# Masked softmax on one core: other store sizes for the last six batches, and the last half store cut at partition 120

## The chip, the cores and the metric

The kernel runs on one core of a Trainium2 chip. The metric is device time in microseconds (us) of one execution, given as the median of seven runs. The profile is of one further execution; its "span" is the time from its first to its last instruction.

## The reference

The input is x of shape 16 x 8 x 256 x 256 (batch, heads, queries, keys) in 32-bit floats, and one length per batch. Along the key axis it is a softmax over the first `length` keys, and zero beyond:

```python
for b in range(batch):
    length = lengths[b]
    masked = x[b, :, :, :length].copy()
    masked = masked - np.max(masked, axis=-1, keepdims=True)
    exp_masked = np.exp(masked)
    result[b, :, :, :length] = exp_masked / np.sum(exp_masked, axis=-1, keepdims=True)
```

The lengths are drawn between 128 and 255. The output is the full 16 x 8 x 256 x 256 array, 33.55 MB, so every batch stores 2 MiB whatever its length.

## The kernel before

A batch has 2048 rows of 256 keys. They are laid on 128 partitions with 16 rows in each (`nt` = 16), so one partition holds 16 KiB of a batch, contiguous in the input and in the output. `half` is 8 of these rows. A tile `xt` has 12 slots of one batch each; batch b lies in slot b modulo 12, and all work is done in place.

Four queues and engines work side by side, and semaphores alone tie them together:

- SP issues the loads of batches 0 to 3 in full width (`load`, L96), then all stores. For each batch it waits on `s_out`, which counts finished half batches, and issues a store of rows 0 to 7 of every partition (8 KiB for each partition), then after a second wait two stores of four rows (4 KiB for each partition): `parts` (L47), the loop at L104 to L110. At the end it waits until the stores of batches 4 to 15, which share one semaphore, have all landed (L111; the profile puts this wait at L96).
- GpSimd (POOL) zeroes the columns from 160 on of the slots 4 to 11, then issues the loads of batches 4 to 15 (L136 to L141). Each load is only as wide as the batch's length, rounded up to one of a few widths (`pick`). For batches 12 to 15 it first waits until the stores of batches 0 to 3, whose slots they take, have landed, by the count `16 * len(parts)` (L140).
- The vector engine (DVE) builds a cap per batch (L167), takes the minimum of x and the cap so that masked keys become very negative (`clip`, L182), and later takes the reciprocal of the row sums (L207) and multiplies by it, half a batch at a time (L209). It takes the minimum of batch b + 1 before the multiplies of batch b. Each multiply raises `s_out` by one.
- The scalar engine (ACT) computes the exponential of one row in each partition at a time with the sum beside it (L225), and raises `s_exp` after each half.

A DMA of SP or of GpSimd is carried out by the core's 16 DMA engines, each of which takes its share of the partitions. Loads stand in one queue (q0 in the profile, those of GpSimd) and stores in another (q1, those of SP, which had the four first loads before them). Every DMA raises its semaphore by 16 in all.

The stores of a batch in the code before:

```python
parts = [slice(0, half), slice(half, half + half // 2), slice(half + half // 2, nt)]
```

Of the kernel before, what the change touches and what calls it, by code (L numbers as in the profile page):

```python
# [21 lines left out]
def kernel(  # L22
# [6 lines left out]
    nc = tc.nc  # L29
    P = nc.NUM_PARTITIONS  # L30

    batch, heads, seq_q, seq_k = x.shape
    rows = heads * seq_q
    assert rows % P == 0
    nt = rows // P
    half = nt // 2

    x_f = x.rearrange("b h q k -> b (h q) k").rearrange("b (p t) k -> b p t k", p=P)
    out_f = out.rearrange("b h q k -> b (h q) k").rearrange("b (p t) k -> b p t k", p=P)

    slots = min(12, batch)
# [2 lines left out]
    widths = list(range(160, 248, 8))  # L44
    low = widths[0]

    parts = [slice(0, half), slice(half, half + half // 2), slice(half + half // 2, nt)]  # L47
    mid = seq_k // 2

    pool = ctx.enter_context(tc.tile_pool(name="all", bufs=1))  # L50
# [1 line left out]
    xt = pool.tile([P, slots, nt, seq_k], F32, name="xt")  # L52
# [12 lines left out]
    inv_sum = pool.tile([P, batch, nt], F32, name="inv_sum")  # L65
    warm = pool.tile([P, 1], F32, name="warm")

    with tc.tile_critical(no_gpsimd_drain=True):  # L68
        sem = lambda n: ctx.enter_context(nc.semaphore(n))
        s_word = sem("s_word")  # L70
        s_word_p = sem("s_word_p")
        s_ones = sem("s_ones")
# [4 lines left out]
        early = batch - slots  # L77
        s_st = [sem(f"s_st{b}") for b in range(early)] + [sem("s_st")] * slots
# [5 lines left out]
        s_out = sem("s_out")  # L84

        def length(engine, b):

            return nc.values_load(  # L88
                (word_p if engine == POOL else word)[0:1, 2 * b : 2 * b + 1],
                engines=[engine],  # L90
                skip_runtime_bounds_check_because="compared with constants, never an address",
            )
# [9 lines left out]
        for b in range(1, ahead):  # L102
            load(nc.sync, b, seq_k)
        for b in range(batch):  # L104
            for k, s in enumerate(parts):
                if k < 2:
                    nc.sync.wait_ge(s_out, 2 * b + k + 1)
                nc.sync.dma_start(
                    out=out_f[b, :, s, :], in_=xt[:, b % slots, s, :]
                ).then_inc(s_st[b], 16)  # L110
        nc.sync.wait_ge(s_st[-1], 16 * len(parts) * slots)  # L111

        def pick(v, b, ws):

            if len(ws) == 1:
                load(nc.gpsimd, b, ws[0])
                return
            m = (len(ws) - 1) // 2  # L120
            with nc.gpsimd.If(v <= ws[m]):  # L121
                pick(v, b, ws[: m + 1])
            with nc.gpsimd.Else():  # L123
                pick(v, b, ws[m + 1 :])
# [11 lines left out]
        for n in range(ahead, batch):  # L136
            if n < slots:
                nc.gpsimd.wait_ge(s_fill, n - ahead + 1)
            else:
                nc.gpsimd.wait_ge(s_st[n - slots], 16 * len(parts))  # L140
            pick(length(POOL, n), n, widths + [seq_k])  # L141


# [56 lines left out]
        for b in range(batch):  # L200
# [3 lines left out]
            for h in range(2):  # L204
                s = slice(h * half, (h + 1) * half)
# [4 lines left out]
                    out=t[:, s, :],  # L210
# [8 lines left out]
        for first, last in ((0, slots), (slots, batch)):  # L219
            with nc.Fori(first, last, 1, engines=[ACT]) as i:  # L220
                nc.scalar.wait_ge(s_min, i + 1)
                slot = i - first
                for j in range(nt):
                    e = xt[:, bass.ds(slot, 1), j, :]
                    ins = nc.scalar.activation(  # L225
                        out=e,
                        in_=e,
# [3 lines left out]
                    if (j + 1) % half == 0:  # L231
                        ins.then_inc(s_exp, 1)


# [1 line left out]
_INS = ['x', 'lengths']  # L236
_OUTS = [((16, 8, 256, 256), 'float32')]
# [25 lines left out]
```

The softmax here doesn't subtract the row's maximum and nothing guards it: scores larger than these inputs give would overflow.

## Time and profile before

| What | Value |
|---|---|
| Median of 7 runs | 158.39 us (158.01 to 158.63) |
| The profiled execution's own time | 158.44 us |
| Its span | 156.1 us |
| Vector engine busy | 121.6 us (78% of the span) |
| Scalar engine busy | 105.2 us (67%) |
| GpSimd busy | 25.0 us (16%) |
| Bytes moved by DMA | 62.11 MB, 398 GB/s in the mean |
| HBM read and written | 28.51 MB and 33.55 MB |
| Stores issued by SP | 16 of 1024 KB and 32 of 512 KB |
| First and last issue of a store | 18.6 us and 137.4 us after the span's start |

The profile's page gives the busy time of each engine, then the span in 40 equal slices in which a digit is the busy share in tenths; the row called DMA is the mean share of the 16 DMA engines. The view of waits says who waited for whom. The view of windows cuts the span into chosen stretches and gives the busy time of each engine in each, and at the end of the row the DMA share and the rate. The trace also keeps a record of every single DMA packet (its start, length, bytes and queue, without the number of the DMA engine).

### The profile page before, as it was taken

The page shows a single profiled execution, that of the slowest core. Times are in us where ns is not written, and L with a number is a line of the kernel's source. Part 1 is how long each engine was busy: PE and PEld are TensorE (multiplying, and loading weights), DVE is VectorE, ACT ScalarE, POOL GpSimd, SP SyncE. Part 2 cuts the span into 40 slices and gives each one's busy share as a digit, 9 for nine tenths or more (in the row PEclk, how much of TensorE's full clock was granted, in tenths as well). Part 3 has the DMA queues.
Part 4 walks back from the last instruction along what each step waited for, and adds up shares of the span by engine and source line. Part 5 has one row for each costly group of instructions (what it writes and reads, how often), then busy time and mean ns, then how long its engine had stood idle before and what let it go on. Part 6 is the DMA issues. An engine that isn't in the chain of part 4 may idle for free.

```text
span 156.1 us, 1177 instructions
## 1 busy us (share of the span) xinstructions
PE 0.2 (0%) x1; PEld 0.1 (0%) x1; DVE 121.6 (78%) x99; ACT 105.2 (67%) x514; POOL 25.0 (16%) x27
## 2 busy tenths in 40 slices
PE   0000000000000000000000000000000000000000
PEld 0000000000000000000000000000000000000000
DVE  2566999999999999949995999997977999910000
ACT  3009999896979797948888497979592989300000
POOL 5995045652002002010000000000000000000000
DMA  4999999999999999999999999999999999999990
GB/s 126 424 441 424 437 357 393 410 435 426 382 402 405 411 426 405 418 408 415 409 412 416 405 415 404 412 419 406 418 441 414 422 423 421 421 426 425 429 396 34
DMA packets 11607, 62.11 MB, mean 398 GB/s; under 512 B 1058, under 2 KB 1154, under 8 KB 8786
## 3 DMA queue, kind: packets, MB, share of 16 engines
q1 hardware_dynamic: 7488, 41.95, 65.7%
q0 software_dynamic: 4112, 20.12, 32.0%
q14 instruction: 5, 0.04, 0.1%
q10 hardware_dynamic: 2, 0.00, 0.0%
HBM read 28.51 MB, written 33.55 MB: 397 GB/s over the span
## 4 chain that ended last, share of the span: by engine, by line
DVE 33%; DMA 29%; issue 12%; POOL 6%; another core or an unknown queue 4%; POOLq 1%; SPq 1%; DVEq 0%
DMA xt<-in_x_dram 29%; DVE xt L209 18%; DVE xt L182 12%; POOL xt L133 4%; POOL xt L96 2%; DVE inv_sum L207 1%; DVE cap L167 1%; POOLq L88 1%; SPq L96 1%; POOLq L121 0%; DVEq L195 0%; POOLq L123 0%; DVEq L194 0%; SPq L258 0%
## 5 line engine op out<-in xcount | busy, mean ns | idle before, releaser
L225 ACT ACTIVATE xt<-xt x256 | 102.3, 401 | 27.3 <-DVE xt L182 27.3
L209 DVE TENSOR_TENSOR xt<-xt,inv_sum 128x2048 f32<-128x2048 f32 x32 | 73.3, 2292 | 1.1
L225 ACT ACTIVATION_READ_ACCUMULATOR xt<-xt x256 | 47.7, 186 | 0.0
L182 DVE TENSOR_TENSOR xt<-xt,cap 128x2048 f32<-128x2048 f32 x16 | 36.6, 2286 | 11.4 <-DMA xt<-in_x_dram 10.9
L96 POOL DMA_DIRECT2D xt<-in_x_dram x12 | 12.7, 1057 | 41.7 <-issue 41.6
L133 POOL MEMSET xt<- 128x1536 f32 x8 | 11.0, 1427 | 0.3 <-DVE iota_h L157 0.3
L167 DVE TENSOR_SCALAR cap<-iota_h,len_s 128x256 f32<-128x256 f32 x16 | 9.3, 587 | 0.0
L207 DVE RECIPROCAL inv_sum<-row_sum 128x8 f32<-128x8 f32 x32 | 6.2, 194 | 0.0
L157 DVE TENSOR_SCALAR iota_h<-iota_i 128x256 f32<-128x256 int32 x1 | 0.3, 295 | 2.6 <-POOL iota_i L127 2.6
L218 ACT ACT_TABLE_LOAD x1 | 1.3, 1283 | 1.5 <-SPq L68 1.5
L126 POOL DMA_DIRECT2D word_p<-in_lengths_dram x1 | 0.6, 636 | 1.1 <-SPq L68 1.1
L161 DVE COPY len_s<-len_f 128x16 f32<-128x16 f32 x1 | 0.2, 175 | 0.4 <-PE len_f L146 0.4
L127 POOL IOTA iota_i<- 128x256 int32 x1 | 0.4, 360 | 0.1
L218 ACT ACTIVATE warm<-const-float32-0.0 128x1 f32<-128x1 f32 x1 | 0.2, 203 | 0.0
L130 POOL MEMSET ones<- 1x128 bf16 x1 | 0.2, 194 | 0.0
L146 PE MATMUL len_f<-len_b,ones 1*128 1x16 bf16 x1 | 0.2, 168 | 3.1 <-DVE len_b L159 3.1
L159 DVE CAST len_b<-word 1x16 bf16<-1x16 int32 x1 | 0.2, 156 | 0.0
L247 POOL MEMSET const-float32-0.0<- 128x1 f32 x1 | 0.1, 99 | 0.2 <-issue 0.2
L146 PEld LDWEIGHTS len_f<-len_b,ones 1*128 1x128 bf16 x1 | 0.1, 100 | 3.1 <-POOL ones L130 3.1
L247 POOL MEMSET const-float32-1.0<- 128x1 f32 x1 | 0.1, 99 | 0.0
L247 POOL MEMSET const-bfloat16-1.0<- 128x1 bf16 x1 | 0.1, 99 | 0.0
L247 POOL MEMSET const-uint8-127<- 128x1 uint8 x1 | 0.1, 99 | 0.0
## 6 DMA issues: line engine op xcount, KB each, us to landing
out_dram<-xt SPq DMA_DIRECT2D x16, 1024.0 KB, 22.1
out_dram<-xt SPq DMA_DIRECT2D x32, 512.0 KB, 22.0
xt<-in_x_dram SPq DMA_DIRECT2D x4, 2048.0 KB, 14.4
xt<-in_x_dram POOLq DMA_DIRECT2D x3, 1728.0 KB, 54.2
xt<-in_x_dram POOLq DMA_DIRECT2D x2, 2048.0 KB, 38.1
xt<-in_x_dram POOLq DMA_DIRECT2D x2, 1600.0 KB, 36.6
xt<-in_x_dram POOLq DMA_DIRECT2D x2, 1280.0 KB, 62.1
xt<-in_x_dram POOLq DMA_DIRECT2D x1, 1792.0 KB, 40.6
```

What stands on the lines that cost most here:

```text
L88: return nc.values_load((word_p if engine == POOL else word)[0:1, 2 * b : 2 * b + 1], engines=[engine], skip_runtime_bounds_check_because= ...
L96: engine.dma_start(out=xt[:, b % slots, :, :w], in_=x_f[b, :, :, :w]).then_inc(s_ld[b], 16)
L126: nc.gpsimd.dma_start(out=word64_p, in_=lengths[None, :]).then_inc(s_word_p, 16)
L127: nc.gpsimd.iota(iota_i, pattern=[[1, seq_k]], base=0, channel_multiplier=0).then_inc(s_iota, 1)
L133: nc.gpsimd.memset(xt[:, b, :, low:], 0.0).then_inc(s_fill, 1)
L167: nc.vector.tensor_scalar(out=cap[:, b % 4, :], in0=iota_h, scalar1=len_s[:, b : b + 1], scalar2=-1.0e30, op0=ALU.subtract, op1=ALU.mult,)
L182: return nc.vector.tensor_tensor(out=t[:, :, lo:hi], in0=t[:, :, lo:hi], in1=cap[:, b % 4, None, lo:hi].to_broadcast([P, nt, hi - lo]), op ...
L207: step(nc.vector.reciprocal(out=inv_sum[:, b, s], in_=row_sum[:, b, s]))
L209: ins = nc.vector.tensor_tensor(out=t[:, s, :], in0=t[:, s, :], in1=inv_sum[:, b, s, None].to_broadcast([P, half, seq_k]), op=ALU.mult,)
L218: nc.scalar.activation(out=warm, in_=nc.const_aps.tensor(0.0, (P, 1), F32), func=EXP)
L225: ins = nc.scalar.activation(out=e, in_=e, func=EXP, accum_out=row_sum[:, bass.ds(i, 1), j],)
L247: nc = _bacc.Bacc("TRN2", target_bir_lowering=False, num_devices=1)
```

## The change

Three things change on SP's queue.

- The cuts of a batch's store depend on the batch. Batches 0 to 9 keep half, quarter, quarter. Batches 10, 11 and 15 are stored in two halves, batches 12 to 14 in one piece. A piece waits for the multiply that makes its last row.
- The second half of batch 15, the very last store, is issued as two: partitions 0 to 119, and partitions 120 to 127.
- The counts waited for follow: in GpSimd's wait for the slots, and in SP's wait at the end.

The line that defines `sem` moves out of the block it stood in, with no effect on what is issued.

```diff
-    parts = [slice(0, half), slice(half, half + half // 2), slice(half + half // 2, nt)]
+    quarter = nt // 4
+    cuts = lambda b: (
+        [0, half, half + quarter, nt]
+        if b < slots - 2
+        else [0, half, nt]
+        if b < slots or b == batch - 1
+        else [0, nt]
+    )
+
+    def parts(b):
+        return [slice(i, j) for i, j in zip(cuts(b), cuts(b)[1:])]
+
+    def groups(b, s):
+        if b == batch - 1 and s.stop == nt:
+            return [slice(0, 120), slice(120, P)]
+        return [slice(0, P)]
...
-            for k, s in enumerate(parts):
-                if k < 2:
-                    nc.sync.wait_ge(s_out, 2 * b + k + 1)
-                nc.sync.dma_start(
-                    out=out_f[b, :, s, :], in_=xt[:, b % slots, s, :]
-                ).then_inc(s_st[b], 16)
-        nc.sync.wait_ge(s_st[-1], 16 * len(parts) * slots)
+            for s in parts(b):
+                nc.sync.wait_ge(s_out, 2 * b + (s.stop - 1) // half + 1)
+                for p in groups(b, s):
+                    nc.sync.dma_start(
+                        out=out_f[b, p, s, :], in_=xt[p, b % slots, s, :]
+                    ).then_inc(s_st[b], 16)
+
+        nc.sync.wait_ge(s_st[-1], 16 * sum(
+            len(groups(b, s)) for b in range(early, batch) for s in parts(b)
+        ))
...
-                nc.gpsimd.wait_ge(s_st[n - slots], 16 * len(parts))
+                nc.gpsimd.wait_ge(s_st[n - slots], 16 * len(parts(n - slots)))
```

More of the change, by code (lines that the diff above doesn't have):

```diff
@@ L66 @@
     warm = pool.tile([P, 1], F32, name="warm")
+    sem = lambda n: ctx.enter_context(nc.semaphore(n))
     with tc.tile_critical(no_gpsimd_drain=True):
-        sem = lambda n: ctx.enter_context(nc.semaphore(n))
         s_word = sem("s_word")
```

## The prediction

> **What bounds the kernel now.** I read the busy shares first, then the row of DMA slices, the waits, the tail in short windows, and last the trace's records of single DMA packets. From the page:
>
> ```profile
> PE 0.2 (0%) x1; PEld 0.1 (0%) x1; DVE 121.6 (78%) x99; ACT 105.2 (67%) x514; POOL 25.0 (16%) x27
> ...
> DMA  4999999999999999999999999999999999999990
> ```
>
> No compute engine is full, but the DMA engines are at nine tenths or more in 38 of 40 slices. The waits of the SP queue say what the end waits for:
>
> ```profile
> SPq L108 <- DVE xt L209: 97.3, 31, 15.4
> SPq L96 <- DMA out_dram<-xt: 15.9, 1, 15.9
> ```
>
> The second row is the final wait: once its last store was issued, SP sat 15.9 us until the stores had landed. The multiplies (L209) are therefore early, and the store backlog sets the end. The issues of the last two batches give its depth:
>
> ```profile
> L108 SPq DMA_DIRECT2D out_dram<-xt x6: 332/547/1121, 129.7 to 137.4; - x6
> ...
> DMA to landing us min/median/max: 15.0/16.2/17.0
> ```
>
> Now the tail. In each row come the stretch, its length, the busy times of the five compute rows, the clock, the DMA share and GB/s:
>
> ```profile
> 142.00:150.00 8.00, 0.00 (x0) 0.00 (x0) 0.00 (x0) 0.00 (x0) 0.00 (x0) 1.00 1.01 423
> ...
> 151.80:152.40 0.60, 0.00 (x0) 0.00 (x0) 0.00 (x0) 0.00 (x0) 0.00 (x0) 1.00 0.64 259
> 152.40:152.90 0.50, 0.00 (x0) 0.00 (x0) 0.00 (x0) 0.00 (x0) 0.00 (x0) 1.00 0.30 123
> 152.90:153.30 0.40, 0.00 (x0) 0.00 (x0) 0.00 (x0) 0.00 (x0) 0.00 (x0) 1.00 0.10 41
> 153.30:153.70 0.40, 0.00 (x0) 0.00 (x0) 0.00 (x0) 0.00 (x0) 0.00 (x0) 1.00 0.08 31
> 153.70:154.10 0.40, 0.00 (x0) 0.00 (x0) 0.00 (x0) 0.00 (x0) 0.00 (x0) 1.00 0.05 20
> 154.10:154.50 0.40, 0.00 (x0) 0.00 (x0) 0.00 (x0) 0.00 (x0) 0.00 (x0) 1.00 0.00 0
> ```
>
> One engine of 16 is a share of 0.06. So the engines run dry from 151.8 us on, two are busy at 153.1 and one alone from about 153.4 to 154.1. The packet records confirm it. Each engine closes its part of a DMA with a 4-byte mark; the last 16 marks start at 151.80 to 152.91 us for fourteen engines, at 153.345 for the fifteenth and at 154.077 for the sixteenth. The same spacing stands in the marks of every batch since about 128 us, and two engines are already about 1.8 us behind the median in the store that ends near 34 us: a lag that stays, not an accident of the last store. From the last mark to the span's end are 2.06 us of closing waits and drains, which the change leaves alone.
>
> [...]exactly two stragglers, and the lag grows between 18 us (last mark 0.4 us after the median) and 34 us, when GpSimd issues its first nine loads. The records carry no engine numbers, so which straggler is which is not shown.[...]
>
> **The change part by part.** Costs per engine come from the marks of one engine in the saturated stretches. Eight rows of 4096 B with their mark take 1.249 us, eight of 8192 B 2.452, and eight of 16384 B 4.862; the last figure is from the four opening loads, no store of that size being in the trace.
>
> *Sizes.* Batches 10 and 11 go from half, quarter, quarter to two halves: 2 x 1.249 - 2.452 = 0.046 us each, 0.092. Batches 12 to 14 become one store each: 2.452 + 2.498 - 4.862 = 0.088, three times 0.264. The last half of batch 15 in rows of 8192 B saves another 0.046. Sum 0.402 us on every engine, on the path, because DMA time is the path there. For the 16384 B store the bounds are 4.95 (no saving, that is 0.264 less) and 4.81 (every fixed cost of 4.6 ns per packet gone as rows double again, some 0.15 more); I take the load's figure.
>
> *Does this reach the loads?* The last load packet starts at 122.5 us and the first packet of batch 10's stores at 122.05, so practically all the resized stores move when the load queue is empty. Sharing between the queues stays as it is, and so do the times at which the vector engine gets its data.
>
> *The added waits.* A whole-batch store waits for the second multiply, about 2.4 us after the first. Behind it on SP are only later stores. Batch 12's rows start to move near 132 us, 13's near 137 and 14's near 142 in the packet records; their second halves are ready at 115.8, 125.1 and 132.2 us. At least 9 us of backlog cover the delay, even when the stores run 0.3 us earlier. Without the cover it would cost 2.4 us once. The reuse of slots, which GpSimd waits for, hangs on batches 0 to 3, whose stores are unchanged; the waits with the new counts therefore cost nothing.
>
> *Issues.* SP issues 41 stores instead of 48, at 0.33 us unblocked. The blocks of up to 5.67 us at a full queue can only shrink. The extra issue of the 8-row piece falls 14 us before its data is needed: nothing.
>
> *The split.* Engine 15 loses its eight rows, 2.452 us. Engines 0 to 14 keep theirs. Engines 0 to 7 take one row and one mark more: 0.306 + 0.009 = 0.31 us.
>
> *Sum.* If the last straggler is number 15 it ends at 154.077 - 0.402 - 2.41 = 151.3 and no longer matters. The second, if it is one of 0 to 7, ends at 153.345 - 0.402 + 0.31 = 153.25; if it is one of 8 to 14, at 152.94. Gain 0.83 or 1.13 us. I take the first[...]. The span goes from 156.14 to 155.31, and the profiled execution from 158.44 to about 157.6; the median shown, 158.39, stands 0.05 lower, so 157.56. I forecast 157.6.
>
> **The rivals.**
>
> *Ports collide (slower).* [...]An engine already draws 4096 B in 155 ns, 26.4 GB/s[...]. It decides from a collision cost of 0.83 us on[...]. For it: 15 is no power of two and every other DMA here has all 128 rows. Against it: nothing in the trace[...]. I take 0 because engines that are out of step[...] meet little of it.
>
> *The wrong engine is freed (same).* If number 15 is not the last straggler, that one keeps its rows: 154.077 - 0.402 + 0.31 = 153.99 when it is among 0 to 7, which gives 158.3; 153.68 when it is among 8 to 14, which gives 158.0.[...]
>
> *The sizes do nothing.* If 16384 B stores take no less than their parts, the gain of the likeliest case drops to 0.57 us, 157.8; still faster.
>
> *The queue runs dry.* A whole-batch store comes too late and the engines idle for up to 2.4 us, 160.0. The 9 us of backlog speak against it.
>
> **How the numbers follow.** Likeliest case, with its 157.2 to 157.9 (the lower end is the second straggler among 8 to 14, the upper the sizes that do nothing plus a little collision): 0.58. Wrong engine 0.16, of which 0.09 lands within 0.2% and 0.07 faster. Ports collide 0.22, of which 0.02 comes out even. Queue dry or something unseen 0.04, split between slower 0.01 and faster 0.03. About 0.2% (0.3 us) is what a measurement of this kernel can tell from no change. Faster 0.68, same 0.11, slower 0.21. The range runs from 157.1 to 158.9: it leaves out most of the collisions and nearly nothing else.[...]
>
> **What would show it.** Right: in the pure-store stretch the batches 12 to 14 pass in 4.86 us each instead of 4.95; the last mark comes at 153.0 to 153.4 us with the second straggler's lag before it; the single-engine share of 0.06 at the very end lasts under 0.5 us; the loads land at the same times up to 122.5 us. Wrong engine: a lone engine still closes the span near 154. Collision: the DMA share stays near one in the last 3 us while GB/s falls well under 400, and single 8192 B rows last markedly longer than their present 309 ns. Queue dry: a DMA share under one between 126 and 150 us. The prediction would also be wrong if the straggler's lag is made anew in each execution, on another engine.

## The result, and the profile after

The changed kernel takes 159.29 us in the median of 26 runs (157.77 to 160.81), the kernel before 158.20 us in the median of 63 (157.77 to 159.54). The ratio is 1.0056, 95% interval 1.0043 to 1.0069: slower by some 0.9 us, where a gain of 0.8 us was forecast. Three runs of the changed kernel, 160.50 to 160.81 us, count as slow, over 1.5% above its fastest, and are left out of the ratio; the others reach 159.97 us.

The profiled execution took 159.59 us, its span is 157.3 us. First the page's busy row and its row of DMA slices:

```profile
PE 0.2 (0%) x1; PEld 0.1 (0%) x1; DVE 120.7 (77%) x99; ACT 105.2 (67%) x514; POOL 25.1 (16%) x27
...
DMA  5999999999999999999999999999999999999960
```

The compute engines do what they did before, and the DMA engines are busy up to the same place; the span has grown behind them. Next the waits of SP:

```profile
SPq L127 <- DVE xt L231: 115.9, 29, 15.5
SPq L115 <- DMA out_dram<-xt: 17.5, 1, 17.5
```

The final wait is 17.5 us in place of 15.9, after a last issue at the same time. The store line in its last stretch and the tail in short windows (stretch, length, five compute rows, clock, DMA share, GB/s), cut like those of before:

```profile
L127 SPq DMA_DIRECT2D out_dram<-xt x4: 332/370/742, 132.0 to 137.3; - x4
```

```profile
142.00:150.00 8.00, 0.00 (x0) 0.00 (x0) 0.00 (x0) 0.00 (x0) 0.00 (x0) 1.00 0.99 420
...
151.80:152.40 0.60, 0.00 (x0) 0.00 (x0) 0.00 (x0) 0.00 (x0) 0.00 (x0) 1.00 0.39 150
152.40:152.90 0.50, 0.00 (x0) 0.00 (x0) 0.00 (x0) 0.00 (x0) 0.00 (x0) 1.00 0.28 115
...
153.70:154.10 0.40, 0.00 (x0) 0.00 (x0) 0.00 (x0) 0.00 (x0) 0.00 (x0) 1.00 0.05 20
154.10:154.50 0.40, 0.00 (x0) 0.00 (x0) 0.00 (x0) 0.00 (x0) 0.00 (x0) 1.00 0.05 20
154.50:154.90 0.40, 0.00 (x0) 0.00 (x0) 0.00 (x0) 0.00 (x0) 0.00 (x0) 1.00 0.05 20
154.90:155.30 0.40, 0.00 (x0) 0.00 (x0) 0.00 (x0) 0.00 (x0) 0.00 (x0) 1.00 0.05 20
155.30:155.70 0.40, 0.00 (x0) 0.00 (x0) 0.00 (x0) 0.00 (x0) 0.00 (x0) 1.00 0.00 0
```

From 151.8 to 152.4 us the share is 0.39 where it was 0.64: most engines now finish earlier, as the smaller number of packets promised, and one has no share of the last half at all. But one engine alone (a share of 0.05 to 0.06) goes on to 155.2 us, where the lone engine of before stopped at 154.1. In this execution the whole loss is on this one engine.

The trace's packet records tell what it did. Its last packets, worked out by joining each packet to the one that starts where it ends (start in us after the span's start, bytes, ns):

```
first half of batch 15, all 128 partitions:
148.745  8192 309      149.051  8192 309      149.356  8192 676      150.038  8192 599
150.642  8192 522      151.161  8192 338      151.495  8192 361      151.853  8192 596
152.465  mark
partitions 0 to 119:   eight of 8192 in 309 each, 152.468 to 154.915, then the mark
partitions 120 to 127: 154.921  8192 309, and the last mark at 155.227
```

It was last before the split began, and yet it takes a share of both pieces. Fifteen of the last marks close the large piece and eight the small one: one engine has neither, and eight take a row more. The prediction assumed these counts. It calls the one 15 and the eight 0 to 7: names for their parts in the split, as no record carries an engine's number. And six of the straggler's packets last 338 to 676 ns where 309 is the usual length, while more and more of the other engines, from 150.33 us on all of them, have gone on to the 120-partition piece. With the straggler's lag taken as it was before, the sum closes: 0.40 us less for the sizes, 0.31 us more for the extra row and its mark, and 1.24 us more in the six slow packets (676 + 599 + 522 + 338 + 361 + 596 - 6 x 309 ns) make 1.15 us; the last mark moved from 154.077 to 155.227. That the lag is the same in two executions isn't shown, so the close fit is partly luck. The engine that the split frees, the only one without a share, set its last mark at 150.146 us. With eight rows more, as in an uncut half, it would have ended 2.452 us later, at 152.60: it was not the one to free.

### The profile page after: what moved, and what is told of

Same layout as the page of the kernel before. It is cut to its first block, busy times and chain, and to the rows that moved or that the text cites. A ratio compares the mean times of both kernels' runs of the same rounds, so it can differ in the third digit from the quotient of the medians.

```text
span 157.3 us, 1169 instructions
## 1 busy us (share of the span) xinstructions
PE 0.2 (0%) x1; PEld 0.1 (0%) x1; DVE 120.7 (77%) x99; ACT 105.2 (67%) x514; POOL 25.1 (16%) x27
## 4 chain that ended last, share of the span: by engine, by line
DMA 33%; DVE 29%; issue 12%; POOL 7%; another core or an unknown queue 5%; POOLq 1%; SPq 1%; DVEq 0%
DMA xt<-in_x_dram 33%; DVE xt L231 16%; DVE xt L204 10%; POOL xt L155 4%; POOL xt L115 2%; DVE inv_sum L229 1%; DVE cap L189 1%; POOLq L107 1%; POOLq L143 1%; SPq L115 1%; DVEq L217 0%; POOLq L145 0%; DVEq L216 0%; SPq L279 0%
## 5 line engine op out<-in xcount | busy, mean ns | idle before, releaser
L189 DVE TENSOR_SCALAR cap<-iota_h,len_s 128x256 f32<-128x256 f32 x16 | 8.4, 531 | 0.0
```

Of the source, the lines that this page charges most:

```text
L189: nc.vector.tensor_scalar(out=cap[:, b % 4, :], in0=iota_h, scalar1=len_s[:, b : b + 1], scalar2=-1.0e30, op0=ALU.subtract, op1=ALU.mult,)
```

## The experiments

Theory A was: the sizes gain what was forecast, and the split loses it, by an extra row on a straggler that it does not free and by packets that collide, at SBUF as I supposed. Theory B: the larger stores are themselves at fault. "Excess" below is the sum, over all packets and engines in the pure-store stretch, of the time beyond the common duration of a packet of that size (309 ns for 8192 B, 611 for 16384 B).

**The sizes without the split.**

```diff
     def groups(b, s):
-        if b == batch - 1 and s.stop == nt:
-            return [slice(0, 120), slice(120, P)]
+        pass
         return [slice(0, P)]
```

> The new store sizes with the last half store left whole. Theory A (the split is the whole loss[...]): the straggler ends 0.40 us earlier than before, span near 155.7, ratio 0.9975. Theory B (the larger stores themselves are slower, or the straggler lags more beside them): no better than before, ratio 1.000 or above, at worst the whole 1.0056.

Measured: 157.60 us (157.49 to 157.89), ratio 0.9959 (0.9946 to 0.9973). Two windows of its tail:

```profile
151.80:152.40 0.60, 0.00 (x0) 0.00 (x0) 0.00 (x0) 0.00 (x0) 0.00 (x0) 1.00 0.27 109
152.40:152.90 0.50, 0.00 (x0) 0.00 (x0) 0.00 (x0) 0.00 (x0) 0.00 (x0) 1.00 0.12 49
152.90:153.30 0.40, 0.00 (x0) 0.00 (x0) 0.00 (x0) 0.00 (x0) 0.00 (x0) 1.00 0.00 0
```

The last mark came at 153.153 us. After 126 us no 8192 B packet took over 327 ns, and in the last 13 us none over 309. Theory B falls: the sizes gain 0.65 us, somewhat more than the 0.40 worked out from the packets. The rest is not explained. The straggler's lag differs from one profile to the next: the last mark stood 0.31 us behind the one before it here and 0.73 us in the kernel before. The split alone, then, costs the difference between 0.9959 and 1.0056, 1.5 us.

**The split without the sizes.**

```diff
-    cuts = lambda b: (
-        [0, half, half + quarter, nt]
-        if b < slots - 2
-        else [0, half, nt]
-        if b < slots or b == batch - 1
-        else [0, nt]
-    )
+    cuts = lambda b: [0, half, nt] if b == batch - 1 else [0, half, half + quarter, nt]
```

> The old sizes for batches 0 to 14, batch 15 in halves with the last half split at 120. Theory A: the split costs what the changed kernel shows without its gain from sizes, 0.31 us for the extra row and about 1.25 us of slowed packets, less 0.05 for the merged quarters: 1.5 us over before, ratio 1.009 to 1.010. Theory B: about as before plus 0.3 us, ratio 1.002 or less.

Measured: 160.13 us (159.91 to 160.38), ratio 1.0122 (1.0100 to 1.0144), 1.9 us over before, where 1.5 were expected. Here 8192 B packets take up to 1311 ns, and the excess is 9.0 us, against 1.7 us in the profiled execution of the changed kernel. The same split thus loses more or less from one case to the next; how the engines happen to stand to each other when they reach it may decide, but no run separates that.

**The last half split at 64.**

```diff
-            return [slice(0, 120), slice(120, P)]
+            return [slice(0, 64), slice(64, P)]
```

> The new sizes, the last half split into partitions 0 to 63 and 64 to 127[...]. [...]2.0 to 2.5 us over the sizes alone, and most 8192 B packets of it last near 600 ns. If only the 15-way hand-out is special: within 0.1 us of the sizes alone and packets at 309 ns.

Measured: 158.76 us (157.87 to 159.99), ratio 1.0040 (1.0015 to 1.0064), about 1.3 us over the sizes alone, and packets of up to 929 ns. It lies between the two expectations. So the loss does not need the cut at 120. The profiled execution was the quickest of the ten, so its excess of 4.5 us is on the low side. The next runs therefore moved the edit into mid-stream, onto a store of 16384 B rows.

**Batch 12 split at 120, in mid-stream.**

```diff
-        if b == batch - 1 and s.stop == nt:
+        if b == 12:
             return [slice(0, 120), slice(120, P)]
```

> The new sizes, the last half store whole, and instead batch 12's store (16384 B rows) split at 120, in mid-stream. If the split costs by collisions: packets of 16384 B well over 611 ns in the stretch 130 to 142 us, the DMA rate falls below 400 GB/s there, and the engines that meet them are late to the end, up to 1.3 us over the sizes alone; engine 15 skips eight rows, 4.9 us, and runs ahead. If the loss needs the end of the kernel: no slow packets, and the end only 0.6 us later than the sizes alone, for the extra 16384 B row on the straggler.

Measured: 162.12 us, ratio 1.0261 (1.0226 to 1.0297), 4.5 us over the sizes alone and far more than was expected. The windows around batch 12, first of the sizes alone:

```profile
132.00:136.00 4.00, 0.00 (x0) 0.00 (x0) 3.96 (x3) 0.98 (x6) 0.00 (x0) 1.00 1.03 442
136.00:140.00 4.00, 0.00 (x0) 0.00 (x0) 0.01 (x1) 0.00 (x0) 0.00 (x0) 1.00 1.00 430
```

and of this run:

```profile
132.00:136.00 4.00, 0.00 (x0) 0.00 (x0) 3.96 (x3) 1.52 (x8) 0.00 (x0) 1.00 1.11 383
136.00:140.00 4.00, 0.00 (x0) 0.00 (x0) 0.56 (x1) 0.00 (x0) 0.00 (x0) 1.00 0.94 279
```

The DMA share stays near one (1.00 and 0.94) while the rate falls from 430 to 279 GB/s: the packets last longer. The excess is 36 us summed over the engines. The loss is the split's own, and does not need the kernel's end. The engines are out of step here as well: their last marks for batch 11 lie between 131.2 and 133.4 us, those for batch 14 in the changed kernel between 146.3 and 148.7. So their spread doesn't explain why the loss is larger here; the store has twice the bytes, and what else makes the difference was not tried.

**On which side is the loss, HBM or SBUF?** Two runs change only the HBM side. In the first all stores have 128 partitions, but batches 12 and 13 lie interleaved in HBM, so that rows are 32 KiB apart. In the second the split in batch 12 stays, but its rows are dealt out in turns, so that the engines write neighbouring rows, if each takes eight consecutive partitions, which was supposed. These extracts of the code, and the next one, show only the lines that make the write's target; in the first and in the next run `groups` gives whole stores.

```diff
...
+                    if b in (12, 13):
+                        pair = out_f[12:14].rearrange("b p t k -> (b p) (t k)")
+                        dst = pair.rearrange("(p c) (t k) -> c p t k", c=2, k=seq_k)[b - 12]
...
```

> The sizes alone, with all stores over 128 partitions; batches 12 and 13 are written interleaved into each other's place, 16 KiB of one and 16 KiB of the other, so that rows of neighbouring partitions lie 32 KiB apart in HBM[...] (these two batches thus land in another order in the output). If the split loses to the write pattern in HBM: slow 16384 B packets in 132 to 142 us like those of the split in batch 12, and 2 us or more over the sizes alone. If it loses at the SBUF side: no slow packets, and the time of the sizes alone, 157.6 us.

```diff
...
+                    if b == 12 and p.start == 0:
+                        dst = dst.rearrange("(i g) t k -> g i t k", g=15)
...
```

> Batch 12 split at 120 in mid-stream as before, but the rows of the large piece go to HBM dealt out in turns (partition 8g + i to row 15i + g)[...] (batch 12 thus lands in another order). SBUF side: the loss stays, excess of the 16384 B packets near the 33 us summed over the engines that the plain split in batch 12 had, time near 162 us. HBM side: most of the loss is gone, below 159.5 us.

Measured: 157.55 us (ratio 0.9967, 0.9952 to 0.9982) for the first, and 162.43 us (1.0273, 1.0245 to 1.0302; two runs) for the second. The window that decides, of the first and then of the second:

```profile
136.00:140.00 4.00, 0.00 (x0) 0.00 (x0) 0.00 (x0) 0.00 (x0) 0.00 (x0) 1.00 1.01 434
```

```profile
136.00:140.00 4.00, 0.00 (x0) 0.00 (x0) 0.32 (x1) 0.00 (x0) 0.00 (x0) 1.00 1.10 258
```

The wider pitch in HBM cost nothing (excess about 0.1 us, as in the sizes alone), and the other order in HBM did not help (45 us). This points to the SBUF side, but by elimination alone: the packet records hold neither partitions nor addresses, so that the first run writes at the distances of the split isn't shown either.

**Batch 12 in one store, its HBM side in 16 groups.** If the HBM side of a 128-partition store is written as 16 groups, and if an engine takes one group, it must read eight consecutive partitions:

```diff
...
+                    if b == 12:
+                        dst = dst.rearrange("(i g) t k -> g i t k", g=16)
...
```

> The sizes alone, and batch 12's store over all 128 partitions and 16 engines, but with its HBM side written as 16 groups of 8 rows (partition 8g + i to row 16i + g, so this batch lands in another order)[...]. If it is the hand-out in consecutive eights that collides at SBUF: slow 16384 B packets in 132 to 142 us, an excess summed over the engines of 30 us or more, time near 162 us. If it takes 15 engines or two pieces to lose: no slow packets and 157.6 us.

Measured: 162.31 us in two runs, ratio 1.0275 (1.0184 to 1.0366), excess 44 us:

```profile
136.00:140.00 4.00, 0.00 (x0) 0.00 (x0) 0.70 (x1) 0.00 (x0) 0.00 (x0) 1.00 1.01 279
```

One store, 128 partitions, and the same fall to 279 GB/s. So the loss needs neither a cut nor a second piece. What the lossy stores have in common may be which partitions an engine reads: an inference, as no record shows them. One rival remains for this run taken alone: with a group to each engine, an engine also writes rows 256 KiB apart, and no store with that stride but without the regrouping was run. The plain split, whose rows are consecutive in HBM, lost as much without it.

**Batch 12 split at 64.**

```diff
...
+        if b == 12:
+            return [slice(0, 64), slice(64, P)]
...
```

> The sizes alone, and batch 12's store split into partitions 0 to 63 and 64 to 127[...]. [...]an excess summed over the engines of 40 us or more when the engines are in step, 2 to 5 us over the sizes alone.[...]

Measured: 162.22 us in two runs, ratio 1.0269 (1.0075 to 1.0463), excess 59 us:

```profile
132.00:136.00 4.00, 0.00 (x0) 0.00 (x0) 3.38 (x3) 0.37 (x2) 0.00 (x0) 1.00 1.09 342
136.00:140.00 4.00, 0.00 (x0) 0.00 (x0) 0.00 (x0) 0.00 (x0) 0.00 (x0) 1.00 1.06 262
140.00:144.00 4.00, 0.00 (x0) 0.00 (x0) 0.00 (x0) 0.00 (x0) 0.00 (x0) 1.00 0.88 295
```

The rate falls as with the cut at 120, to 262 GB/s. The two runs, 161.02 and 163.41 us, are 3.4 and 5.8 us over the sizes alone, where 2 to 5 were expected if the split loses, and 157.6 us without slow packets if it does not. At its usual 4.862 us, batch 12 takes 16 engines 78 us of DMA time in all (an estimate from the packet times). The excess is three quarters of that here, and about half with the cut at 120 (36 and 45 us) and with the 16 groups (44 us). What sets these shares was not tried.

**Who is last?** First by cutting the eight-row piece of the changed kernel into seven rows and one, then, with hardly any split data, by storing only the last of batch 15's 16 rows in pieces (its cuts become 0, 8, 15, 16; that line is not shown).

```diff
-            return [slice(0, 120), slice(120, P)]
+            return [slice(0, 120), slice(120, 127), slice(127, P)]
```

> The changed kernel with its eight-row piece cut into partitions 120 to 126[...] and 127[...]. If the straggler is number 7, it gets no extra row: after its eight rows of the large piece no packet follows on it, and the kernel ends 0.31 us earlier than the changed kernel, ratio to before about 1.004. If it is one of 0 to 6: as the changed kernel, 1.006, with an extra row on the last engine.

```diff
...
+        if b == batch - 1 and s.start == nt - 1:
+            return [slice(0, 105), slice(105, 113), slice(113, 120), slice(120, P)]
...
```

> The sizes alone, with the last of the 16 rows of batch 15 cut off and stored in pieces of 105, 8, 7 and 8 partitions[...], 1024 B per partition. The number of marks that an engine sets after the large store tells who it is[...]. If the straggler is 7: three marks close its list. If it is 15: it ends with the large store. If it changes from one execution to the next: anything. Time within 0.5 us of the sizes alone.

The first gave 159.45 us, ratio 1.0081 (1.0061 to 1.0100), and tells nothing of the engine: its profiled execution was the quickest of five, 158.03 us, and had no engine standing apart from the others. The second took 158.12 us, ratio 1.0009 (0.9997 to 1.0021): even 128 KiB in four small pieces cost back the gain of the sizes, 0.8 us by the ratios where at most 0.5 was expected. In its trace the last engine ends with these records:

```
152.914  7168 272      153.182  7168 272      153.450  mark      (128 partitions)
153.456 to 153.710     seven of 1024, then a mark at 153.753     (105 partitions)
153.759  1024  mark    153.807  1024  mark    153.855  1024  mark
```

Four marks after the large store: it has a row of each small piece, that of seven partitions included. So it is not the engine that this piece leaves out, called 7 in the expectation. In the changed kernel's trace the straggler was one of the eight with an extra row. In neither execution, then, was the engine without a share of a split, called 15, the last. In the other traces the last engine isn't told.

**Full-width loads.** Is the lag made by GpSimd's many small load packets?

```diff
-            pick(length(POOL, n), n, widths + [seq_k])
+            load(nc.gpsimd, n, seq_k)
```

> The sizes alone, with every load of GpSimd at full width: 16 KiB runs, 128 data packets per load in place of some 350, and 33.55 MB read in place of 28.5 (the result is unchanged). If the straggler's lag comes from GpSimd's many small load packets and their descriptors: in the closing stretch no engine is more than 0.6 us behind the next. If it is a property of the engine: a lag of 0.7 us or more again. The kernel itself is some 12 us slower for 5.05 MB more at 420 GB/s.

Measured: 165.69 us in two runs, 7.7 us over the kernel before, where some 12 were expected. In the last stores no engine was more than 0.4 us behind the next, as the first theory has it. But from about 30 to 90 us the last engine of each store was 1.4 us behind the median, with full-width loads too, and the lag shrank only from 95 us on, when the load queue stood empty for 6.4 us; it was still 0.9 us at the end. The small packets alone do not make it. What makes it stays open.

**One store each from batch 10 on.**

```diff
...
+    cuts = lambda b: [0, half, half + quarter, nt] if b < slots - 2 else [0, nt]
...
```

> No split, batches 0 to 9 as before, batches 10 to 15 in one store each. By the marks another 2 x 2.452 - 4.862 = 0.042 us saved on each of the batches 10, 11 and 15, 0.13 us less than the sizes alone: 157.5 us, ratio 0.995. If a store as late as batch 15's cannot wait for its second half: later than the sizes alone by up to 2.4 us.

Measured: 157.45 us (157.26 to 158.16), ratio 0.9957 (0.9943 to 0.9971). It beats both kernels, and can't be told from the sizes alone. Batch 15 in a single store doesn't come too late.

## Why the prediction was wrong

*What bounds the kernel: right.* The end is set by the slowest DMA engine (its last mark at 155.227 us, in a span of 157.3), and the loads and SP's issues moved as forecast. The last load packet starts at 122.3 us (122.5 before), SP's longest block at an issue fell from 5.67 to 2.09 us, and the DMA share shows no gap in the stretch after 126 us.

*The sizes: right in mechanism, a little small.* Whole-batch stores follow each other in 4.862 us on an engine, as worked out from the loads. Alone they gained 0.65 us (0.43 to 0.85), forecast 0.40.

*Slips that move nothing.* SP issued 40 stores, not 41. Two of the sixteen last marks belong to the quarter store before: by engine the first fourteen end at 151.74 to 152.91 us, not from 151.80. And the freed engine's sum should take off 2.45, not 2.41.

*The split's hand-out of engines: right.* Fifteen marks for the large piece and eight for the small one are in the trace, and one engine has neither. Which partitions an engine of the large piece reads no trace shows; there, by the inference above, the loss lies.

*"If the last straggler is number 15": the first step that failed.* I had two stragglers without numbers and took the later one for the engine that the split frees, which no trace showed. The straggler of the changed kernel was one of the eight with a row more. The rival of the wrong engine had this sum, 153.99 us for the last mark; without slow packets it would have been 155.227 - 1.24 = 153.99. So the split gained nothing, and an extra row of 0.31 us was paid.

*"I take 0" for the collisions: the second, and the one that decides the sign.* In the trace the slow packets cost the straggler 1.24 us; by the runs the split costs 1.5 us, of which the extra row is 0.31. The rival, that engines hinder each other in the split store, had the sign; that ports are where they meet was an assumption, and no trace shows it. In the profiled execution the other engines lost little (excess 0.5 us outside the straggler, most of it one packet of 722 ns), while the late one, still at its rows of the 128-partition store, lost the 1.24 us. That those ahead held it up is inferred from the times alone. Of the signs named for a collision only the long 8192 B rows came; the DMA share did not stay near one in the last 3 us (0.39 from 151.8 to 152.4 us). My reason for taking 0, that engines out of step meet little, is refuted by the runs in mid-stream, where engines as far out of step lost 36 us together. The reason against the rival, that nothing in the trace shows it, was no reason: in the kernel before, every DMA of size has 128 partitions, so the trace could not show it.

The range ended at 158.9 because the collisions were given 0.22. With a loss of unknown size on one side and a gain of 0.8 us on the other, and nothing in the trace to weigh them by, that was a guess, and too low.

## What to carry to other kernels

Keep the large DMAs of a DMA-bound kernel at all 128 partitions, and don't regroup their HBM side: here a regrouped store of all 128 lost as much as a cut one (162.31 and 162.12 us, against 157.60). A cut along the partitions cost 1.5 us at the end and 4.5 us in mid-stream, perhaps because it gives the engines other partitions to read, while a cut along the rows costs 0.05 us by the packet times. When the queue ahead of them holds several microseconds of stores, 9 or more here, let the stores grow; here that gained 0.65 us. Before work is taken off the engine that is last, find out which it is: small pieces mark it in the trace, as the four marks did here.

## What the runs showed of the hardware

- A store of 16384 B rows moves at the pace of the loads of that size: 4.862 us for eight rows on an engine, against 4.950 for the same bytes as half, quarter, quarter.
- The same 2 MiB from the same 128 partitions move at 430 GB/s or, with their HBM side in 16 groups, at 279 GB/s in the slowest of the four-microsecond windows, with a DMA share near one in both (1.00 and 1.01). So the share does not tell the rate.
- A 128-partition store still under way on a late engine was slowed too, while the others were in the 120-partition piece: its packets of 309 ns took up to 676.
